# Loading the mixer's output weights ahead of a modulation group, and moving conv taps and weight splits from VectorE to GpSimd

## The chip, the cores and the metric

The kernel runs on one core of one Trainium2 chip. The metric is device time in microseconds, the median over runs.

## The reference

One call computes a first block (batch 1, 512 positions, model width 1024), then two further layers with attention (8 forgetting heads and 8 sparse heads), each with a gated feed-forward. The change touches the first block most:

```
cond = silu(c) @ ada_w + ada_b          # shift1, scale1, gate1, shift2, scale2, gate2
h = modulate(rmsnorm(x), shift1, scale1)
u, v, val, gate = split(h @ w_in + b_in)
y_a = gelu(u) * spatial(layernorm(gelu(v)))            # chunks of 128 positions
y_b = silu(channel_norm(conv31(val * sigmoid(gate))))  # causal depthwise conv, 512 channels
y = concat(rmsnorm(y_a), rmsnorm(y_b))
x = x + gate1 * (y @ w_out)
h2 = modulate(rmsnorm(x), shift2, scale2)
x = x + gate2 * ((silu(h2 @ w_gate) * (h2 @ w_up)) @ w_down)
```

All weights and activations are float32.

## The kernel before

**Activations** stand transposed: 1024 channels are eight tiles of 128 partitions, 512 positions are the free axis. `X0` to `X3` hold the residual (two channel tiles each), `H0` to `H7` the operand of the next matmul, each with a hi part (written by ACT) and a lo part (by DVE).

**Products.** Each float32 product is three matmuls: hi weight by hi and by lo activation, lo weight by hi activation. `Weights` (`W`) does the weights: `plan` queues a slab's spec, `load` (L299 to L318) issues one DMA of 512 KB into `raw`, and `split` lets ACT copy it to `wh` and DVE subtract to get `wl`; with the flag `pool` of the spec, GpSimd subtracts. `take` hands out a slab and then keeps `look` = 4 ready; `ahead(n)` loads and splits until n are ready. All slabs share a ring of 37 buffers with other tiles, so that a load can wait for a buffer to come free; SP's queue issues the DMAs in order.

**Modulation.** `ada_fetch` issues slabs of ada_w (`adaw`, 512 KB); `ada_group` uses eight of them, 32 small matmuls, ends with `adasb` and a transposing pair, and fetches ahead for the next group. Groups run once after `spatial`, then at m == 2 and m == 5 of the loop over w_out's first half (called second and third group).

**The conv** runs two channel tiles at a time over 31 lags. In `conv`, lags below `nd` are DVE operations into PSUM (`ax`), the others an ACT scale into `tap` (two buffers) and a GpSimd addition into `cv`. `center` then adds `ax` to `cv` on DVE, and statistics, `z`, silu and H4 to H7 follow.

**The output projection.** The loop over m takes slabs 0 to 3 of w_out (rows of H0 to H3); the second half takes slabs 4 to 7 (H4 to H7) by halves of 256 positions, adds into X, sums squares (`sq`, `st`), and `normed` makes H0 to H7 of the next norm from X and the reciprocal `rsw`. Then the first feed-forward begins with the tiles of gate and up, of 24 matmuls each.

**Order.** Parts outside `Ordered` are placed by a scheduler; a wrapper at L113 records every instruction, so that the rows of the profile all read L113 and are told apart by tile names. `uT` is the gated spatial part, from which H0 to H3 come; `sp` its PSUM-side operand.

Of the kernel before, what the change touches and what calls it, by code (L numbers as in the profile page):

```python
# [48 lines left out]
BK = 0  # L49
HP = 300  # L50
ND0 = 23
ND1 = 17
ND = (ND0, ND1)
PP0 = 1
PP1 = 6
# [3 lines left out]
PP5 = 2  # L59
PP = (PP0, PP1, PP2, PP3, PP4, PP5)  # L60
WP = 0
UP = 0
PY = 4
PZ = 4
GNV = False
# [55 lines left out]
def body(ctx: ExitStack, tc: tile.TileContext, I: dict, out, dbg=None):  # L121
# [28 lines left out]
    def MM():  # L150
        return ps.tile([P, S], F32, tag="mm", name="mm", bufs=4)
# [186 lines left out]
    W = Weights(4)  # L338
    W.pool = True

    def rows_of(w, k0, kt, c0, n):
        return w[k0 * P:(k0 + kt) * P, c0:c0 + n].rearrange("(k p) m -> p k m", p=P)

    def plan_cols(w, k0, kt, c0, n):
        W.plan([(0, P, 0, n, rows_of(w, k0, kt, c0, n))], kt, n)
# [9 lines left out]
    for c in range(4):  # L355
        plan_cols(w_in, 0, 8, c * P, P)
    for k0 in (0, 4):
        for g in range(4):
            plan_cols(I["w_out"][0], k0, 4, g * HS, HS)

# [15 lines left out]
    def plan_ffn(gate, up, down, pool=False):  # L376
        def gu(m):
            plan_cols(gate, 0, 8, m * P, P)
            plan_cols(up, 0, 8, m * P, P)

        def dn(m, k0, kts):
            for kt in kts:
                plan_cols(down, k0, kt, m * P, P)
                k0 += kt
        for m in range(KF0 + 1):
            W.pool = pool and m < 4
            gu(m)
        for m in range(KD - 1):
            dn(m, 0, (7, 7))
        for m in range(KF0 + 1, KF):  # L390
            gu(m)
        dn(KD - 1, 0, (7, 7))
        for m in range(KD):
            dn(m, KF0, (8,))

    plan_ffn(I["w_ffn_in"][0][:, :FF], I["w_ffn_in"][0][:, FF:], I["w_ffn_out"][0], UP)

    awi = I["attn_w_in_2"][0]
    FQ, FK, FV, FFG, NQ, KC, VC, KS, VS, KW, VW, NG = 0, 512, 1024, 1536, 1544, 2056, 2184, 2312, 2440, 2568, 2696, 2824
    plan_cols(awi, 0, 8, KC, P)  # L400
    plan_cols(awi, 0, 8, VC, P)
    plan_cols(awi, 0, 8, KS, P)
    plan_cols(awi, 0, 8, KW, P)
    for k0, kt in ((0, 3), (3, 3), (6, 2)):
        W.plan([(0, P, 0, 128, rows_of(awi, k0, kt, VS, 128)), (0, P, 128, 256, rows_of(awi, k0, kt, VW, 128)),
                (0, P, 256, 264, rows_of(awi, k0, kt, FFG, 8)), (0, P, 264, 288, rows_of(awi, k0, kt, NG, 24))], kt, 288)
# [206 lines left out]
    def pump(n, m=0):  # L613
        owed[0] += n
        owed[1] += m
        n, m = int(owed[0]), int(owed[1])
        owed[0] -= n
        owed[1] -= m
        for j in range(max(n, m)):
            if j < m and bp:  # L620
                bp.popleft()()
            if j < n and bg:
                bg.popleft()()
# [25 lines left out]
    def ada_group(ahead):  # L649

        pq = MM()
        for k in range(KD):
            ada_fetch(1)
            a, col, bias, _ = adal.popleft()
            for j in range(4):
                TE.matmul(pq[32 * j:32 * j + 32, :HS], lhsT=c32[:, k, :], rhs=a[:, j // 2, (j % 2) * HS:(j % 2 + 1) * HS],
                          start=(k == 0), stop=(k == KD - 1))
        ada_columns(pq, col, bias)
        ada_fetch(ahead)
# [265 lines left out]
    def factor(acc_, bank=ST):  # L925

        rsb = ACC()
        act(rsb, stats(acc_, 0, S, 512, bank=bank), AF.Copy)
        return rsb
# [243 lines left out]
    def out_mm(o, k0, slab, e, c0, c1):  # L1173
        wh, wl, _ = slab
        cs = slice(e * P, (e + 1) * P)
        for k in range(4):
            HO.mm3(o, k0 + k, wh[:, k, cs], wl[:, k, cs], c0, c1, k == 0, k == 3)

    def gated(m, o, c0, c1, rsb, eng):
        t = T()[:, :c1 - c0]  # L1180
        stt(t, o, mod[:, 16 + m:17 + m], rsb[:, c0:c1], OP.mult, OP.mult)
        eng.tensor_tensor(x_(m, c0, c1), x_(m, c0, c1), t, op=OP.add)
# [10 lines left out]
    for m in range(KD):  # L1193
        oa.append(MM())
        out_mm(oa[m], 0, gets(m // 2)[0], m % 2, 0, S)
        if m == LA:
            fa = factor(accA)
        if m >= LA:
            for x in range(0 if m == LA else m, m + 1):
                gated(x, oa[x], 0, S, fa, G if GA else V)  # L1200
        pump(PY, PP[5])
        if m in (2, 5):
            ada_group(ADN if m == 2 else 2)
    pump(len(bg))
# [575 lines left out]
```

## Time and profile before

| | before |
|---|---|
| median of 3 runs | 1676.74 us (1675.54 to 1678.24) |
| profiled execution | 1677.02 us |
| its span | 1675.3 us |
| PE, DVE, ACT, POOL busy | 1635.3, 882.7, 680.8, 129.3 us |
| granted TensorE clock, mean | 0.993 of full speed |

PE is TensorE's matmuls, DVE VectorE, ACT ScalarE, POOL GpSimd, SP the engine that issues most DMAs. Times in the rows are counted from the span's start. The profiled execution is 1.72 us longer than its span.

### The profile page before, as it was taken

The numbers are of one execution on the slowest core, as the hardware profiler recorded it, in microseconds if no ns is written. First come the engines' busy times: TensorE is split into PE (matmuls) and PEld (weight loads), VectorE is DVE, ScalarE is ACT, GpSimd is POOL, SyncE is SP. The second block draws the span as 40 slices with busy tenths as digits, with TensorE's granted clock in tenths as the row PEclk, the third lists the DMA queues.
The fourth block names the chain that finished last, engine by engine and source line by source line (L and its number), as shares of the span: only waits on it lengthen the run. The fifth ranks groups of instructions, "written<-read, shape, count | busy, mean of one in ns | idle before, by whom it ended". The sixth has DMA issues, their size and how long they took to land.

```text
span 1675.3 us, 22098 instructions
## 1 busy us (share of the span) xinstructions
PE 1635.3 (98%) x8797; PEld 1361.0 (81%) x8797; DVE 882.7 (53%) x1645; ACT 680.8 (41%) x1232; POOL 129.3 (8%) x144
## 2 busy tenths in 40 slices
PE   7999999999999999999999999999998999999998
PEld 4885798887888998777778988888887998888886
DVE  5798584444333584778766444323258734441244
ACT  4685352222222364455557323213236822322232
POOL 0452000000000011100101000000012100000002
PEclk9999999999999999999999999999999999999999
DMA  9634445544532433311134232234221532232511
GB/s 304 178 129 174 151 113 176 158 145 126 157 96 63 111 67 79 89 39 39 38 101 126 68 97 76 88 113 139 88 76 51 139 89 76 76 125 90 150 39 51
DMA packets 245168, 179.55 MB, mean 107 GB/s; under 512 B 20688, under 2 KB 220224, under 8 KB 245064
## 3 DMA queue, kind: packets, MB, share of 16 engines
q1 hardware_dynamic: 240520, 176.99, 36.0%
q10 hardware_dynamic: 4544, 1.14, 0.4%
q8 instruction: 69, 1.13, 0.3%
q14 instruction: 35, 0.29, 0.1%
HBM read 175.99 MB, written 2.11 MB: 106 GB/s over the span
## 4 chain that ended last, share of the span: by engine, by line
PE 86%; DVE 3%; ACT 2%; DMA 1%; issue 1%; SPq 0%; DVEq 0%; ACTq 0%
PE mm L113 79%; PE st L113 3%; PE ax L113 3%; DVE wl L113 0%; DVE pw L113 0%; DMA raw<-in_w_out_dram 0%; ACT pw L113 0%; ACT sq L113 0%; DVE H L113 0%; DVE XT L113 0%; DMA raw<-in_ffn_w_up_dram 0%; ACT pt L113 0%; DVE mg L113 0%; DVE lg L113 0%; DVE fk L113 0%
## 5 line engine op out<-in xcount | busy, mean ns | idle before, releaser
L113 PE MATMUL mm<-H,wh 128*128 128x512 f32 (+1 forms) x3168 | 872.6, 362 | 8.2 <-ACT wh L113 2.9
L113 PEld LDWEIGHTS mm<-H,wh 128*128 128x128 f32 x3168 | 566.2, 190 | 105.6 <-issue 5.4
L113 PE MATMUL mm<-H,wl 128*128 128x512 f32 (+1 forms) x1584 | 569.5, 361 | 3.0 <-DVE wl L113 2.9
L113 DVE TENSOR_TENSOR wl<-raw,wh 128x1024 fp32r<-128x1024 f32 (+1 forms) x257 | 309.4, 1220 | 217.5 <-ACT wh L113 202.3
L113 PEld LDWEIGHTS mm<-H,wl 128*128 128x128 f32 x1584 | 300.5, 190 | 47.9 <-DVE wl L113 3.6
L113 ACT ACTIVATE wh<-raw 128x1024 fp32r<-128x1024 f32 (+1 forms) x257 | 262.1, 1041 | 121.1 <-PE mm L113 49.1
L113 PE MATMUL mm<-wh,hid 128*128 128x512 f32 x704 | 217.5, 389 | 0.0
L113 DVE TENSOR_TENSOR silu<-silu,mm 128x512 f32<-128x512 f32 (+1 forms) x77 | 47.0, 611 | 249.3 <-PE mm L113 245.3
L113 PEld LDWEIGHTS mm<-wh,hid 128*128 128x128 f32 x704 | 132.1, 188 | 27.4
L113 ACT ACTIVATE hid<-silu 128x512 fp32r<-128x512 f32 (+1 forms) x77 | 43.8, 569 | 242.2 <-DVE silu L113 234.5
L113 PE MATMUL mm<-wl,hid 128*128 128x512 f32 x352 | 137.3, 390 | 0.0
L113 PE MATMUL mm<-hid,wh 128*128 128x512 f32 (+1 forms) x464 | 116.3, 340 | 0.0
L113 PEld LDWEIGHTS mm<-hid,wh 128*128 128x128 f32 x464 | 80.3, 190 | 9.9 <-issue 0.4
L113 POOL TENSOR_TENSOR mg<-mg,gb 128x512 f32<-128x512 f32 x32 | 44.2, 1387 | 467.0 <-ACT sq L113 458.4
L113 ACT ACTIVATE silu<-silu 128x512 f32<-128x512 f32 (+1 forms) x52 | 29.3, 565 | 123.3 <-DVE silu L113 123.2
L113 PE MATMUL mm<-hid,wl 128*128 128x512 f32 (+1 forms) x232 | 79.1, 341 | 0.0
L113 PEld LDWEIGHTS mm<-wl,hid 128*128 128x128 f32 x352 | 66.1, 188 | 13.8 <-DVE wl L113 0.3
L113 DVE TENSOR_TENSOR silu<-mm,rsb 128x512 f32<-128x512 f32 (+1 forms) x52 | 31.6, 608 | 73.1 <-PE mm L113 72.6
L113 PE MATMUL mm<-wh,H 128*128 128x512 f32 (+2 forms) x256 | 66.0, 345 | 2.8 <-ACT wh L113 1.6
L113 DVE TENSOR_TENSOR hid<-silu,hid 128x512 fp32r<-128x512 f32 (+1 forms) x77 | 47.3, 614 | 37.4 <-ACT hid L113 37.3
L113 POOL TENSOR_TENSOR cv<-cv,tap 128x488 f32<-128x488 f32 (+12 forms) x40 | 52.5, 1347 | 87.3 <-ACT cv L113 70.3
L113 ACT ACTIVATE silu<-mm 128x512 f32<-128x512 f32 (+1 forms) x25 | 13.7, 546 | 110.4 <-PE mm L113 110.4
(271 smaller groups left out, 1634.9 us busy)
## 6 DMA issues: line engine op xcount, KB each, us to landing
adaw<-in_ada_w_dram SPq DMA_DIRECT2D x48, 512.0 KB
raw<-in_w_ffn_in_dram SPq DMA_DIRECT2D x44, 512.0 KB
raw<-in_ffn_w_gate_dram SPq DMA_DIRECT2D x44, 512.0 KB
raw<-in_ffn_w_up_dram SPq DMA_DIRECT2D x44, 512.0 KB
raw<-in_ffn_w_down_dram SPq DMA_DIRECT2D x44, 512.0 KB
raw<-in_w_in_dram SPq DMA_DIRECT2D x16, 512.0 KB
adaw<-in_ada_f_w_dram SPq DMA_DIRECT2D x16, 512.0 KB
raw<-in_attn_w_in_dram SPq DMA_DIRECT2D x16, 512.0 KB
```

Of the source, the lines that this page charges most:

```text
L113: ins = f(*a, **k)
```

## The change

`ND1` goes from 17 to 14: for the second pair of channel tiles, lags 14, 15 and 16 of each tile move from DVE to ACT and GpSimd. `W.ahead(6)` ahead of the second group puts slabs 4 to 7 of w_out ahead of the slabs which that group fetches for the third. The flag `pool` is set for w_out's slabs 4 to 7, for the gate and up slabs of m < 4 of the first feed-forward (`UP` = 1) and for four slabs of the attention's input projection.

```diff
-ND1 = 17
+ND1 = 14
...
-UP = 0
+UP = 1
...
     for k0 in (0, 4):
+        W.pool = k0 == 4
         for g in range(4):
             plan_cols(I["w_out"][0], k0, 4, g * HS, HS)
...
+    W.pool = True
     plan_cols(awi, 0, 8, KC, P)
     plan_cols(awi, 0, 8, VC, P)
     plan_cols(awi, 0, 8, KS, P)
     plan_cols(awi, 0, 8, KW, P)
+    W.pool = False
...
         pump(PY, PP[5])
+        if m == 2:
+            W.ahead(6)
         if m in (2, 5):
             ada_group(ADN if m == 2 else 2)
```

SP's queue from the first w_out slabs to the first feed-forward slabs, as the difference of the two orders (L309 is `load`, L636 or L639 `ada_fetch`):

```order
 L309 DMA raw<-in_w_out_dram 128x4x256 x4
-L636 DMA adaw<-in_ada_w_dram 128x1024 x8
-L309 DMA raw<-in_w_out_dram 128x4x256 x2
-L636 DMA adaw<-in_ada_w_dram 128x1024 x8
-L309 DMA raw<-in_w_out_dram 128x4x256 x2
+L639 DMA adaw<-in_ada_w_dram 128x1024 x8
+L309 DMA raw<-in_w_out_dram 128x4x256 x4
+L639 DMA adaw<-in_ada_w_dram 128x1024 x8
```

Slabs 6 and 7 have moved ahead of the third group's eight `adaw` slabs.

DVE where H3 of the mixer is made, as the difference (`ax_1175` and `ax_1213` are the two tiles of the pair, `wl_1222` is slab 3, `H3_93` the lo part):

```order
 L113 SCALAR_TENSOR_TENSOR ax_1175<-glu_291,fixed_69,ax_1175 128x499
+L113 SCALAR_TENSOR_TENSOR ax_1213<-glu_291,fixed_69,ax_1213 128x499
+L113 TENSOR_TENSOR cv_289<-cv_289,ax_1175 128x512
+L113 TENSOR_TENSOR wl_1222<-raw_1219,wh_1221 128x1024
 L113 SCALAR_TENSOR_TENSOR H3_93<-uT_1043,fixed_69,H3_93 128x512
-L113 SCALAR_TENSOR_TENSOR ax_1213<-glu_291,fixed_69,ax_1213 128x499
-L113 TENSOR_TENSOR wl_1222<-raw_1219,wh_1221 128x1024
 L113 TENSOR_TENSOR acc_1260<-acc_1260,sq_1324 128x512
```

The addition of the first tile's `ax` into `cv`, which waits for GpSimd's last tap of that tile, and slab 3's split now stand ahead of H3's lo part.

PE where the first feed-forward begins, first before (`mm_2148` and `mm_2149` are the first gate and up tile, `mm_2216` the next gate tile):

```order
L113 MATMUL mm_2148<-H5_95,wh_1743 128x256
L113 MATMUL mm_2148<-H5_95,wl_1744 128x256
L113 MATMUL mm_2149<-H4_94,wl_1750 128x256
L113 MATMUL mm_2149<-H5_95,wh_1749 128x256 x2
L113 MATMUL mm_2149<-H5_95,wl_1750 128x256
L113 MATMUL mm_2216<-H0_90,wh_1755 128x256 x2
L113 MATMUL st_1946<-sq_2120,fixed_69 128x256
L113 MATMUL mm_2148<-H6_96,wh_1743 128x256
L113 MATMUL mm_2149<-H6_96,wh_1749 128x256
L113 MATMUL mm_2216<-H0_90,wl_1756 128x256
```

and of the change (`mm_2160` is the first gate tile, `mm_2161` the first up tile):

```order
L113 MATMUL mm_2160<-H5_95,wh_1755 128x256 x2
L113 MATMUL mm_2160<-H5_95,wl_1756 128x256
L113 MATMUL mm_2160<-H6_96,wh_1755 128x256 x2
L113 MATMUL mm_2160<-H6_96,wl_1756 128x256
L113 MATMUL mm_2160<-H7_97,wh_1755 128x256
L113 MATMUL mm_2161<-H0_90,wh_1761 128x256
L113 MATMUL mm_2160<-H7_97,wh_1755 128x256
L113 MATMUL mm_2160<-H7_97,wl_1756 128x256
```

The first gate tile is no longer interleaved with the next two; one matmul of another tile is left among its last ones.

## Rows read from the trace of the kernel before

**Rows 1.** The page's first line and its busy time by engine (share of the span, instructions).

```profile
span 1675.3 us, 22098 instructions
PE 1635.3 (98%) x8797; PEld 1361.0 (81%) x8797; DVE 882.7 (53%) x1645; ACT 680.8 (41%) x1232; POOL 129.3 (8%) x144
```

**Rows 2.** The timeline of PE: start, us, engine, operation, and in brackets the idle time before with what released it. The last row is from 383 to 389 us, the others from 189.9 to 204.

```profile
194.53 0.70 PE L113 MATMUL st<-sq,fixed 128*128 128x256 f32 x2 [0.50 <-ACT sq L113]
198.10 1.01 PE L113 MATMUL mm<-H,wh 128*128 128x256 f32 x3 [2.87 <-ACT wh L113]
...
201.04 0.63 PE L113 MATMUL mm<-H,wh 128*128 128x256 f32 x2
...
201.68 0.63 PE L113 MATMUL mm<-H,wh 128*128 128x256 f32 x2
...
385.19 0.79 PE L113 MATMUL mm<-H,wl 128*128 128x512 f32 x1 [2.86 <-DVE wl L113]
```

**Rows 3.** The chain of waits that ended last, between 176 and 206 us: start, us, what.

```profile
188.79 1.43 SPq L636
...
190.27 6.70 DMA raw<-in_w_out_dram
...
196.99 1.06 ACT wh L113
```

**Rows 4.** Windows: from and to, length, busy time (instructions) of PE, PEld, DVE, ACT and POOL, granted PE clock, DMA share, GB/s.

```profile
190.90:204.00 13.10, 9.73 (x49) 8.59 (x49) 6.24 (x14) 3.45 (x6) 0.00 (x0) 0.75 0.71 208
204.00:230.00 26.00, 25.88 (x194) 24.84 (x193) 23.01 (x45) 13.34 (x26) 0.00 (x0) 1.00 0.36 101
230.00:240.00 10.00, 10.00 (x85) 10.00 (x84) 8.17 (x16) 6.18 (x11) 0.00 (x0) 1.00 0.40 110
```

**Rows 5.** The timeline of SP's queue, which issues the slabs, 120 to 200 us.

```profile
137.80 2.21 SPq L309 DMA_DIRECT2D raw<-in_w_out_dram  x2
178.08 12.14 SPq L636 DMA_DIRECT2D adaw<-in_ada_w_dram  x8
190.27 0.98 SPq L309 DMA_DIRECT2D raw<-in_w_out_dram  x2
```

**Rows 6.** The timeline of PE, 137 to 191 us.

```profile
140.65 0.50 PE L113 MATMUL mm<-H,wh 128*128 128x512 f32 x1 [1.29 <-DVE H L113]
...
142.67 0.58 PE L113 MATMUL mm<-H,wh 128*128 128x512 f32 x1
...
150.67 1.66 PE L113 MATMUL mm<-H,wh 128*128 128x512 f32 x6
...
185.78 0.95 PE L113 MATMUL ax<-fixed,acc 128*128 128x1 f32 x8
...
187.29 0.49 PE L113 MATMUL ax<-fixed,rs 128*128 128x128 f32 x2
```

**Rows 7.** The timeline of ACT, 128 to 164 us.

```profile
139.32 1.27 ACT L113 ACTIVATE tap<-glu,fixed 128x482 f32<-128x482 f32 x2
...
145.62 0.36 ACT L113 ACTIVATE adasb<-mm 128x256 f32<-128x256 f32 x1
```

**Rows 8.** The timeline of DVE, 128 to 192 us.

```profile
134.76 3.38 DVE L113 TENSOR_TENSOR uT<-uT,sp 128x512 f32<-128x512 f32 x2
138.07 0.74 DVE L113 SCALAR_TENSOR_TENSOR sp<-mm,fixed,bvs 128x512 f32<-128x512 f32 x1
...
143.41 0.68 DVE L113 TENSOR_TENSOR uT<-uT,sp 128x512 f32<-128x512 f32 x1
...
149.19 0.75 DVE L113 SCALAR_TENSOR_TENSOR H<-uT,fixed,H 128x512 fp32r<-128x512 f32 x1
...
150.50 1.22 DVE L113 TENSOR_TENSOR wl<-raw,wh 128x1024 fp32r<-128x1024 f32 x1
...
162.19 0.68 DVE L113 TENSOR_TENSOR cv<-cv,ax 128x512 f32<-128x512 f32 x1
```

**Rows 9.** The timeline of POOL, 118 to 164 and 609 to 617 us, and from the page the group of its `mg` operations (busy, mean ns of one).

```profile
129.56 1.04 POOL L113 TENSOR_TENSOR cv<-cv,tap 128x485 f32<-128x485 f32 x1 [5.95 <-ACT tap L113]
132.37 5.22 POOL L113 TENSOR_TENSOR cv<-cv,tap 128x484 f32<-128x484 f32 x4 [1.77 <-ACT tap L113]
140.15 2.79 POOL L113 TENSOR_TENSOR cv<-cv,tap 128x482 f32<-128x482 f32 x2 [2.55 <-ACT tap L113]
...
615.01 0.39 POOL L113 CAST ks<-ks 64x256 fp32r<-64x256 f32 x1 [472.07 <-ACT ks L113]
...
L113 POOL TENSOR_TENSOR mg<-mg,gb 128x512 f32<-128x512 f32 x32 | 44.2, 1387 | 467.0 <-ACT sq L113 458.4
```

**Rows 10.** The timeline of DVE, 194 to 238 us.

```profile
213.93 1.74 DVE L113 RECIPROCAL rsw<-sdw 128x256 f32<-128x256 f32 x1
215.59 1.16 DVE L113 TENSOR_TENSOR wl<-raw,wh 128x1024 fp32r<-128x1024 f32 x1
...
232.44 0.38 DVE L113 SCALAR_TENSOR_TENSOR H<-t,fixed,H 128x256 fp32r<-128x256 f32 x1
```

**Rows 11.** The timeline of PE, 203.5 to 238 us.

```profile
212.67 0.70 PE L113 MATMUL st<-sq,fixed 128*128 128x256 f32 x2
...
217.58 0.70 PE L113 MATMUL st<-sq,fixed 128*128 128x256 f32 x2
...
218.24 0.40 PE L113 MATMUL mm<-H,wh 128*128 128x256 f32 x2
```

## The prediction

> **What bounds the kernel now.** I read the share of each engine first [rows 1]: PE is busy for 1635.3 of 1675.3 us, so whatever is to be won lies in PE's idle time, its clock, or work taken from it, and this change takes no work from PE. I therefore listed PE's idle pieces in the stretch that the change rearranges, 120 to 240 us. The largest stands at 198.10, 2.87 us behind an ACT split [rows 2]; 0.50 us stands at 194.53. The chain around that stall [rows 3] names its origin: SP's queue is busy issuing the third modulation group's slabs until 190.22, the output slab of w_out is issued only at 190.27, takes 6.70 us to land, and its split by ACT ends at 198.05. Last the windows by stage [rows 4]: from 190.9 to 204 the granted clock averages 0.75, from 204 on it is 1.00. The PE rows after the stall show the lower of the two levels, 1.2 GHz: a matmul of 256 columns starts every 0.21 us at 201.04 to 201.68 where it starts every 0.12 us from 230 to 240.
>
> So the late slab costs 0.50 + 2.87 us idle, and the 5.8 us from 198.1 to 203.9 at half clock do the work of 2.9 us: **6.3 us in all**, out of 40 that PE is idle in the whole span.
>
> **W.ahead(6).** SP's queue is in order. Before, slabs 6 and 7 stand behind the third group's eight `adaw` slabs, and the first of those waited until 178.08 [rows 5]. In the changed order all of w_out precedes them. Slab 5 now waits for a buffer until the second add into X1 (before: issued at 137.80), which stands on DVE behind the normalised conv output, about 174; slabs 6 and 7 follow about 176 and 177, the group's slabs from 178, as before. At 12.14 us for eight [rows 5], 1.5 each, the six that this group's result needs have been issued by 187, and PE wants the last near 190. Slabs 5 to 7 are needed from 192 on and are then 14 us old. I count the whole 6.3 us: **-6.3**. If the slabs were again late by as much, it would be 0.
>
> One smaller loss comes with it. In the changed PE order the group's 24 matmuls no longer stand around the `ax` statistics, so that between the sums and the broadcast of their reciprocal nothing fills the way over ACT and DVE: the sums ended at 186.73, the broadcast began at 187.29 [rows 6]; with the hand-over back to PE **+0.7**.
>
> **Three more taps a tile on Pool.** This takes six operations from DVE and puts six ACT taps of 0.64 us and six Pool adds into 137 to 155 [rows 7, 9]. What matters is order. On ACT, four taps now stand between `adasb` (ends 145.98 [rows 7]) and the split of slab 3 and the hi part of H3. On DVE the addition `cv<-cv,ax`, which needs Pool's last tap of its tile, now stands ahead of slab 3's split and of the lo part of H3; before it came at 162.19, long after Pool had finished at 142.94 [rows 8, 9]. By hand: taps on ACT from 146.0 to 148.5; their Pool adds take 1.04 us alone to 1.31 (5.22 for four) beside DVE [rows 9], first one from 146.6, so the fourth ends at 150.8 to 151.9; then the addition 0.6, the split 1.15 (1.22 less what overlaps [rows 8]), at worst another Pool add of 1.0 in between, and H3's lo 0.75: 153.3 to 155.4, instead of 149.94. PE has 13 matmuls that don't need it, 0.23 us each from 150.67, hence until 153.7 [rows 6]. The stall is 0 to 1.7 us; I take **+1.1**, nearer to the end with Pool and DVE in each other's way, because that is how these rows look now (uT below). PE was sent to half clock here once already, at 142.67, after a wait of 1.29 us at 140.65 [rows 6]; if it happens again it costs another 1.5.
>
> Slab 3's load now waits for the third uT addition (about 144.1) and the second group's eight slabs stand behind it, the third of them behind the acc addition after H3 (155.4). PE uses that one about 161 and the others 2 us apart, against 1.5 us on the queue. I cost it at nothing; by a landing of 6.70 us [rows 3] it would be 1.
>
> **Splits on Pool.** The order shows 16: four of w_out, eight of the first feed-forward slabs, four in the attention input. Price of one: the trace has no 128x1024 operation on Pool. Two taps of 485 columns are 2.1 us; two `mg` of 128x512 at 1.387 are 2.8 [rows 9]. I take 2.4, against 1.21 on DVE [rows 8]. Pool is empty from 142.94 to 615.01 [rows 9], so its own time is free; what isn't is DVE's. `uT<-uT,sp`, two operands in SBUF, takes 1.69 us each while Pool adds taps and 0.68 after; `sp<-mm`, with one operand in PSUM, keeps 0.74 at 138.07 beside it [rows 8]. So a DVE operation with two SBUF operands loses about 1.0 us to a Pool add of 1.31: three quarters of it, 1.85 us of a split of 2.4.
>
> The Trainium skill, "SBUF — State Buffer", section "SBUF: two separate sides", is stricter: the port pair is an exclusive lock, and the one that starts second waits for the other's whole instruction. By that, each split costs the full 2.4.
>
> Where this counts is the way to the first feed-forward matmul. Before, DVE is busy without a gap from the reciprocal at 213.93 to H7's lo part at 232.82 [rows 10], 18.9 us, of which four splits like that at 215.59 take 1.1 each and a second reciprocal 1.7 like the first; the changed order has neither ahead of H7, which leaves 12.8. PE before had 24 matmuls of the next tile `mm_2149` and some of `mm_2216` to fill the waits for H4 to H7; in the changed order `mm_2160` stands alone, with one matmul of fill. From the last statistics matmul to H7's use PE has 104 matmuls at 0.118 and 7 `st` at about 0.54 (0.66 from 217.58 to 218.24 with one matmul [rows 11]), 16.1 us; the reciprocal started 1.3 after that point (212.67 [rows 11] to 213.93), so DVE has 14.8 us for 12.8: slack 2.0. Three Pool splits fall into it: the first beside the reciprocal, 0.7 of it left over, two others 1.85 each, 4.4; less 2.0 is **+2.4**. By the quoted rule it is 0.7 + 4.8 - 2.0 = 3.5, and the sum would be 1.1 higher. If Pool blocks nothing it is 0; if all three block 2.8 in full, 6.4.
>
> The w_out and later feed-forward splits are loaded four slabs ahead and I cost them at nothing; PE takes 2.9 us for a 24-matmul slab, longer than Pool needs. Nor the attention's four: PE shows no idle there that a split ends; without that cover 4 x 1.2 = 4.8. The second large stall, 385.19 [rows 2], stays: the order there is the same.
>
> **Sum.** -6.3 + 0.7 + 1.1 + 2.4 = -2.1. On the profiled execution (1677.02, of which 1675.3 is the span [rows 1]) that is 1674.9; the median shown is 0.28 lower, so **1674.6**.
>
> **Rivals.**
> - *The slab gain arrives whole*: Pool blocks DVE for less than the 2.0 us of slack, H3 is in time. -6.3 + 0.7 to 1.1: 1671 to 1672, at most 1673.3. For it: ten splits at 1.22, 12 us, leave DVE where it is full. Chance 0.36.
> - *Slower, by the port*: the three splits around H3 to H7 block in full, 8.4 - 2.0 = 6.4, and the waiting sends PE to half clock as at 198.10, 2.9 more. -6.3 + 0.7 + 1.1 + 9.3 = +4.8: 1681.5. It decides once those splits hold DVE for over 7 us with the clock down. For it: the lone `mm_2160`; against: three in a row must each hit a two-operand instruction. Chance 0.16, with what the same mechanism does in the second half's H chain.
> - *The change doesn't do what it says*: slabs 6 and 7 wait for X buffers until about 185 and the group is later too; 0 + 0.7 + 1.1 + 2.4 = +4.2: 1680.9. Against: the queue orders them by adds that run at 174 to 177. Chance 0.06.
> - *My case*, given back in part, 1673.4 to 1678: chance 0.42.
>
> **Numbers.** A measurement of this kernel tells about 0.2% (3.35 us) from nothing: below 1673.4 is faster, above 1680.1 slower. Faster 0.36, same 0.43, slower 0.21. The range takes in the whole gain (-5.6 with one loss, 1671) and stops at 1681, short of the port's worst.
>
> **What would show it.** Right: no wait for `wh` near 198 and granted clock 1.00 from 190 to 205; `raw<-in_w_out_dram` issued x4 ahead of the third group; a PE wait for DVE H near 154; `wl` on Pool at 2.1 to 2.8 us and X, t or H on DVE at up to 2 us beside it; PE waits for DVE H of some 2 us in sum ahead of the first 24 matmuls of the feed-forward. Wrong: a PE wait for `adaw` near 160 or 190, a half-clock stretch behind H3 or H7, or DVE at its own pace beside Pool's splits.

## The result and the profile after

| | before | after |
|---|---|---|
| median | 1676.14 us (6 runs) | 1691.29 us (1687.55 to 1696.53, 6 runs) |
| profiled execution, its span | 1677.02, 1675.3 us | 1691.96, 1690.2 us |

The ratio is 1.0093 with a 95% interval of 1.0076 to 1.0110: the change makes the kernel slower by 13 to 18 us. I had forecast 1674.6 with a range that ended at 1681.

The page of the changed kernel, its first line, the busy time by engine, and the group of GpSimd's splits (busy, mean ns of one, idle before):

```profile
span 1690.2 us, 22130 instructions
...
PE 1640.7 (97%) x8797; PEld 1363.7 (81%) x8797; DVE 887.1 (52%) x1623; ACT 685.4 (41%) x1238; POOL 178.3 (11%) x166
...
L113 POOL TENSOR_TENSOR wl<-raw,wh 128x1024 fp32r<-128x1024 f32 x16 | 40.0, 2501 | 409.0 <-ACT wh L113 409.0
```

Sixteen splits left DVE, and DVE is busy for 4.4 us **longer** than in [rows 1], although sixteen splits of 1.22 and six taps are gone from it. That is the first sign: other DVE operations became longer by more than what was taken away. PE is idle for 49.5 us in place of 40.

The windows of the changed kernel, in the columns of [rows 4]:

```profile
160.00:181.40 21.40, 21.40 (x154) 13.55 (x147) 10.97 (x17) 7.52 (x12) 1.90 (x1) 0.88 0.47 164
...
190.90:204.00 13.10, 9.81 (x87) 6.40 (x86) 2.36 (x7) 2.19 (x4) 2.36 (x1) 0.81 0.96 335
204.00:230.00 26.00, 22.50 (x157) 21.11 (x157) 19.22 (x34) 11.18 (x21) 9.56 (x4) 0.96 0.34 87
```

From 160 to 181.4 the granted clock is 0.88; before, the same window reads:

```profile
160.00:181.40 21.40, 21.40 (x142) 14.10 (x142) 16.73 (x26) 8.89 (x14) 0.00 (x0) 1.00 0.11 33
```

From 204 to 230 PE lacks 3.5 us of work where it lacked 0.12 in [rows 4]. The timeline of PE names what it waits for:

```profile
151.65 0.73 PE L113 MATMUL mm<-H,wh 128*128 128x512 f32 x2 [1.11 <-DVE fixed L113]
...
156.17 0.50 PE L113 MATMUL mm<-H,wh 128*128 128x512 f32 x1 [1.27 <-DVE H L113]
...
190.33 0.39 PE L113 MATMUL mm<-H,wh 128*128 128x256 f32 x1 [2.71 <-DVE H L113]
...
197.55 0.64 PE L113 MATMUL mm<-adaw,fixed 128*32 128x256 f32 x8 [1.13 <-DMA adaw<-in_ada_w_dram]
...
201.72 0.69 PE L113 MATMUL st<-fixed,adasb 128*128 128x128 f32 x2 [0.51 <-ACT adasb L113]
...
215.00 0.70 PE L113 MATMUL st<-sq,fixed 128*128 128x256 f32 x2 [1.08 <-ACT sq L113]
...
226.64 0.70 PE L113 MATMUL st<-sq,fixed 128*128 128x256 f32 x2 [1.68 <-ACT sq L113]
...
399.59 0.50 PE L113 MATMUL mm<-H,wl 128*128 128x512 f32 x1 [2.86 <-DVE wl L113]
```

Three marks of PE's timeline make a ledger. The first two rows are of the kernel before, the next two of the change: the start of w_out's second half, and the first matmul with slab 5.

```profile
181.40 0.40 PE L113 MATMUL mm<-H,wh 128*128 128x256 f32 x2
190.91 0.49 PE L113 MATMUL mm<-H,wh 128*128 128x256 f32 x2
```

```profile
186.27 0.40 PE L113 MATMUL mm<-H,wh 128*128 128x256 f32 x2
202.06 0.78 PE L113 MATMUL mm<-H,wh 128*128 128x256 f32 x2
```

The second half of w_out began at 181.40 before and begins at 186.27: 4.9 late. The first matmul with slab 5 began at 190.91 before and begins at 202.06: 11.2 late. The stall behind DVE's split stood at 385.19 [rows 2] and stands at 399.59: 14.4 late, of the 14.9 by which the spans differ. So nearly all of the loss arises between 137 us and the first tiles of the feed-forward, in three stretches: the conv's end (+4.9), the third group (+6.3), and the H chain (from X to the H of the next norm), where the 6.3 us of slab 6's stall went away and 9.5 came in their place.

DVE beside GpSimd, first GpSimd's splits, then DVE's operations of the same times:

```profile
179.50 2.76 POOL L113 TENSOR_TENSOR wl<-raw,wh 128x1024 fp32r<-128x1024 f32 x1 [23.93 <-ACT wh L113]
183.42 2.95 POOL L113 TENSOR_TENSOR wl<-raw,wh 128x1024 fp32r<-128x1024 f32 x1 [1.17 <-ACT wh L113]
187.34 2.39 POOL L113 TENSOR_TENSOR wl<-raw,wh 128x1024 fp32r<-128x1024 f32 x1 [0.96 <-ACT wh L113]
...
223.08 2.38 POOL L113 TENSOR_TENSOR wl<-raw,wh 128x1024 fp32r<-128x1024 f32 x1 [3.85 <-ACT wh L113]
```

```profile
179.97 2.83 DVE L113 TENSOR_TENSOR acc<-acc,sq 128x512 f32<-128x512 f32 x1
182.73 0.74 DVE L113 SCALAR_TENSOR_TENSOR t<-mm,fixed,acc 128x512 f32<-128x512 f32 x1
...
184.05 2.87 DVE L113 TENSOR_TENSOR acc<-acc,sq 128x512 f32<-128x512 f32 x1
...
187.45 2.83 DVE L113 SCALAR_TENSOR_TENSOR H<-cv,fixed,H 128x512 fp32r<-128x512 f32 x1
...
212.40 0.48 DVE L113 SCALAR_TENSOR_TENSOR t<-mm,fixed,acc 128x256 f32<-128x256 f32 x1 [2.06 <-PE mm L113]
...
223.23 2.51 DVE L113 SCALAR_TENSOR_TENSOR t<-X,fixed,rsw 128x256 f32<-128x256 f32 x1
```

Four of these rows (179.97, 184.05, 187.45, 223.23) are DVE operations with two operands in SBUF that start during a split of GpSimd. Each ends 0.3 to 0.55 us after the split: H of 0.75 us takes 2.83, `t` of 0.47 takes 2.51. The `t` at 212.40, with one operand in PSUM (`mm`), keeps its 0.48 during a split that runs from 211.82 to 214.22. PE's wait of 2.71 us at 190.33 is that H. The waits for `st<-sq` are the same thing one step on: an add into X that waited for GpSimd, or stood on DVE behind an operation that did, its square on ACT, and PE behind the square. There are six of them from 210 to 239 us, 6.4 us in sum.

### The profile page after: what moved, and what is told of

Read it like the earlier page. It is cut to its first block, busy times and chain, and to the rows that moved or that the text cites. A ratio compares the mean times of both kernels' runs of the same rounds, so it can differ in the third digit from the quotient of the medians.

```text
span 1690.2 us, 22130 instructions
## 1 busy us (share of the span) xinstructions
PE 1640.7 (97%) x8797; PEld 1363.7 (81%) x8797; DVE 887.1 (52%) x1623; ACT 685.4 (41%) x1238; POOL 178.3 (11%) x166
## 4 chain that ended last, share of the span: by engine, by line
PE 81%; DVE 6%; ACT 2%; issue 1%; DMA 1%; SPq 0%; DVEq 0%; ACTq 0%
PE mm L113 75%; PE st L113 3%; PE ax L113 3%; DVE H L113 1%; DVE t L113 1%; DVE X L113 1%; ACT sq L113 1%; DMA adaw<-in_ada_w_dram 1%; DVE acc L113 0%; DVE wl L113 0%; DVE pw L113 0%; ACT H L113 0%; ACT pw L113 0%; DVE lg L113 0%; DVE XT L113 0%
## 5 line engine op out<-in xcount | busy, mean ns | idle before, releaser
L113 DVE TENSOR_TENSOR wl<-raw,wh 128x1024 fp32r<-128x1024 f32 (+2 forms) x241 | 291.5, 1226 | 207.8 <-ACT wh L113 182.9
L113 POOL TENSOR_TENSOR wl<-raw,wh 128x1024 fp32r<-128x1024 f32 x16 | 40.0, 2501 | 409.0 <-ACT wh L113 409.0
L113 POOL TENSOR_TENSOR cv<-cv,tap 128x488 f32<-128x488 f32 (+15 forms) x46 | 61.9, 1377 | 90.6 <-ACT cv L113 70.3
```

What stands on the lines that cost most here:

```text
L113: ins = f(*a, **k)
```

## The experiments

All times below are medians beside the medians of before on the same chip, with the interval of the ratio.

| kernel | median | before | ratio (95%) |
|---|---|---|---|
| no_pool | 1680.12 | 1675.80 | 1.0023 (1.0011 to 1.0035) |
| no_taps | 1689.67 | 1675.80 | 1.0092 (1.0072 to 1.0111) |
| no_ahead | 1690.10 | 1675.80 | 1.0088 (1.0070 to 1.0106) |
| ahead_only | 1679.78 | 1675.80 | 1.0025 (1.0015 to 1.0035) |
| no_ffn_pool | 1684.98 | 1675.72 | 1.0048 (1.0034 to 1.0062) |
| no_wout_pool | 1685.61 | 1676.31 | 1.0054 (1.0042 to 1.0066) |
| attn_pool_only | 1676.70 | 1676.31 | 1.0008 (0.9997 to 1.0018) |
| taps_only | 1679.47 | 1676.31 | 1.0019 (1.0009 to 1.0029) |
| dummy_sub | 1694.30 | 1675.72 | 1.0106 (1.0091 to 1.0122) |
| dummy_after | 1675.30 | 1676.31 | 0.9991 (0.9979 to 1.0002) |
| dummy_set | 1684.09 | 1675.72 | 1.0046 (1.0033 to 1.0059) |
| fetch_split | 1672.94 | 1675.72 | 0.9974 (0.9963 to 0.9984) |

**Undoing one part.** `no_pool` is the change without every `W.pool` line and with `UP = 0`; `no_taps` has ND1 = 17; `no_ahead` lacks the two lines of `W.ahead(6)`; `ahead_only` is before with those two lines alone.

```diff
+        if m == 2:
+            W.ahead(6)
         if m in (2, 5):
```

> The change without its 16 splits on GpSimd: three more taps a tile and the early load of slabs 4 to 7 stay. Theory P (GpSimd's splits hold DVE's operations with two SBUF operands): the wait of 2.71 us for H at 190.33 and the waits for st<-sq and H from 207 to 242 go, some 11 us: 1680. Theory T (the taps make everything late): only 3 us come back, 1688. Theory A (the early load makes the third group late): 1686 to 1688.

> The change with ND1 = 17 again: GpSimd's splits and the early load stay. Theory P: only the lateness that stands before the first split goes, 4.9 us by the start of the second half of w_out (186.27 against 181.40): 1686.5. Theory T: 1675 to 1678, as nothing is late any more. Theory A: 1686.

> The change without W.ahead(6): slabs 6 and 7 stand behind the third group again. Theory A: the waits for adaw at 197.55 to 200.14 and what follows go, and the time falls to 1680 or below. Theories P and T: the stall for slab 6 comes back, but is partly hidden behind the other waits: 1690 to 1695.

> Before, with W.ahead(6) alone. Theories P and T, and the sum of the prediction: -6.3 for slab 6's stall and its half clock, +0.7 for the statistics without fill: 1670.5. Theory A: the slabs put ahead of the third group make PE wait for adaw instead: 1676 to 1682.

Without the splits on GpSimd 4.3 us are left of some 15: these splits cost 11 in the medians, as theory P has it (in the two profiled executions the stall near 385 stands 15.5 us apart, 384.11 and 399.59). Neither undoing the taps nor undoing the early load brings back more than 2 us of the median. For `no_taps` all three forecasts missed (1675 to 1686.5, measured 1689.67); its profiled execution, the fastest of five, stands at 393.02 at the stall, 6.6 us ahead of the change, so what the taps cost inside the change stays open. And `ahead_only` contradicts P and me: it is 4.0 us slower than before, not 5.6 faster. Its SP queue; slab 6's issue in a narrower window; two pieces of its chain of waits; and PE:

```profile
137.49 43.94 SPq L309 DMA_DIRECT2D raw<-in_w_out_dram  x4
181.48 4.88 SPq L636 DMA_DIRECT2D adaw<-in_ada_w_dram  x8
```

```profile
177.59 0.37 SPq L309 DMA_DIRECT2D raw<-in_w_out_dram  x1
```

```profile
180.34 0.70 DVE acc L113
...
181.06 0.37 SPq L309
```

```profile
188.24 0.64 PE L113 MATMUL mm<-adaw,fixed 128*32 128x256 f32 x8 [1.22 <-DMA adaw<-in_ada_w_dram]
...
194.95 0.69 PE L113 MATMUL st<-fixed,adasb 128*128 128x128 f32 x2 [0.50 <-ACT adasb L113]
...
383.99 0.79 PE L113 MATMUL mm<-H,wl 128*128 128x512 f32 x1 [2.86 <-DVE wl L113]
```

The queue stands ahead of slab 6 until an add into X on DVE is done (issue at 177.59), then ahead of slab 7 until DVE's addition `acc` ends at 181.04 (issue at 181.06), and reaches the third group at 181.48 in place of 178.08 [rows 5]. PE waits for one `adaw` after the other, 3.3 us in sum, and comes to slab 5 at 195.29, 4.4 later than before. From there to the stall at 383.99 it needs 188.7 us in place of 194.3: **the 6.3 us that I read off were there, all but 0.7, and 4.4 of them were paid ahead.** In `no_pool` it is 188.0, the whole 6.3, after an arrival 5.2 late.

At that mark `ahead_only` is 1.2 us ahead of before; its span is 1.7 us longer. Matched row by row with before, its lag goes from -1.2 to +0.1 between 385.19 and 390.0, and from +0.8 to +2.1 between 692 and 702.5: both times around a wait of PE, with the lower clock behind it. What sets the length of these stretches stays open, and so does how much of the 4.0 us of the medians they explain.

**Which splits.** `no_ffn_pool` is the change with `UP = 0`, `no_wout_pool` the change without `W.pool = k0 == 4`, `attn_pool_only` before with the attention's flag alone.

> The change with UP = 0: the first feed-forward's eight splits go back to DVE; w_out's four and the attention's four stay on GpSimd. If GpSimd's splits cost where they stand, the waits for st<-sq from 207 to 242 go and the wait of some 2.7 us for H before the ax sums stays: 1682 to 1685, between the change (1691) and the change without any split on GpSimd (1680). If w_out's splits are the whole cost: 1690. If the feed-forward's are: 1680.

> The change with w_out's slabs 4 to 7 split on DVE again; the feed-forward's eight and the attention's four stay on GpSimd. Without the feed-forward's eight it was 1685.0, without any 1680.1. If the parts add up, w_out's four cost some 5 us beside the attention's share and this gives 1686; if the feed-forward's eight alone are enough for the whole loss, since the same PE waits follow: 1690.

> Before with the four attention slabs on GpSimd alone. The prediction costs them at nothing: 1676. If they hold DVE as the others do: 4 x 1.9 us of waiting DVE, of which PE shows at most a part: 1677 to 1680.

Beside the 4.3 us of `no_pool`, w_out's four (with the attention's) make 9.3, the feed-forward's eight (with the attention's) make 9.3 too: 5.0 each, and the two make 10 of the 11, each uncertain by some 3 us by the intervals. The attention's four are 0.4 us, not to be told from nothing. So the splits cost where DVE's adds and H operations are on PE's way, on average about 1.2 us for each of w_out's and 0.6 for each of the feed-forward's, and nothing that shows for the attention's.

**The taps alone.**

```diff
-ND1 = 17
+ND1 = 14
```

> Before with ND1 = 14 alone. The prediction's term was +1.1: 1677. By the rows of the change, PE stands 4.9 us later at the start of w_out's second half (186.27 against 181.40), and nothing after it gives this back: 1680 to 1681. If PE then waits for the third group or slab 6 in any case and the lateness is absorbed: 1676 to 1677.

Slower by 3.2 us (1.5 to 4.9), more than the prediction's term or its absorption, less than the reading from the rows of the change. The timeline of PE in `taps_only`:

```profile
149.15 0.50 PE L113 MATMUL mm<-H,wh 128*128 128x512 f32 x1 [1.09 <-DVE H L113]
...
152.48 0.73 PE L113 MATMUL mm<-H,wh 128*128 128x512 f32 x2 [1.11 <-DVE fixed L113]
...
156.99 0.50 PE L113 MATMUL mm<-H,wh 128*128 128x512 f32 x1 [1.25 <-DVE H L113]
...
200.93 0.62 PE L113 MATMUL mm<-H,wh 128*128 128x256 f32 x3 [1.48 <-ACT wh L113]
...
385.52 0.50 PE L113 MATMUL mm<-H,wl 128*128 128x512 f32 x1 [2.86 <-DVE wl L113]
```

Three waits in place of the one that I had priced, and DVE's rows at the first two say why:

```profile
147.40 1.69 DVE L113 SCALAR_TENSOR_TENSOR H<-uT,fixed,H 128x512 fp32r<-128x512 f32 x1
149.02 1.71 DVE L113 TENSOR_TENSOR acc<-acc,sq 128x512 f32<-128x512 f32 x1
150.65 1.70 DVE L113 TENSOR_TENSOR uT<-uT,sp 128x512 f32<-128x512 f32 x1
```

GpSimd's later taps hold three more operations, of H2, acc and uT, for a microsecond each. They make the second half of w_out 4.2 us late (185.61 against 181.40). But in this execution the lateness is gone again by the stall near 385 (385.52, before 385.19): the wait for slab 6 shrank from 2.87 to 1.48 us, without the stretch at the lower clock. So the absorbed reading is right up to there, and where the median's 3.2 us arise stays open. Taps (+3.2) and early load (+4.0) together make +4.3, not 7.2, in the medians. The traces fit that, since both make PE late at the same place: the first matmul with slab 5 comes 4.2 us late with the taps, 4.4 with the early load, and 5.2 with both.

**Is it the port, or the late `wl`?** In `dummy_sub` DVE makes every split as before, and GpSimd computes the same subtraction into a tile that nobody reads. `dummy_after` has GpSimd busy in the same places, reading only eight columns of SBUF each time. In both, PE, DVE and ACT have the order of before, instruction by instruction.

```diff
+                    V.tensor_tensor(fl(wl), fl(raw), fl(wh).bitcast(F32), op=OP.subtract)
+                    if pool:
+                        G.tensor_tensor(dummy[:, :n], fl(raw), fl(wh).bitcast(F32), op=OP.subtract)
```

In `dummy_after` the last line is instead:

```diff
+                        G.tensor_copy(dummy[:, :8], fl(wh)[:, :8].bitcast(F32))
+                        for _ in range(2):
+                            G.memset(dummy[:, :n], 0.0)
```

> Before, with DVE making every split as before, and GpSimd computing the same subtraction a second time into a tile that nobody reads, for w_out's slabs 4 to 7 and the feed-forward's first eight. Nobody waits for GpSimd's result. Theory P, the port: DVE's operations with two SBUF operands still wait for whole GpSimd operations, and DVE has its splits besides: 1686 or more. Theory L (what costs is that wl comes 2.4 us after wh and not 1.2, and later): 1676 to 1677, as before.

> As dummy_sub, in the same places, but GpSimd copies eight columns of wh (which makes it wait for ACT's split) and then sets the unread tile to zero twice: busy at the same time, hardly reading SBUF. PE, DVE and ACT have the order of before. If DVE is held by GpSimd's operands: 1676 to 1679, as before. If any GpSimd operation that writes SBUF holds DVE: towards dummy_sub's 1694.

> As dummy_sub, but GpSimd sets the tile to zero twice in place of the subtraction, so that it is busy and reads no SBUF. Theory P with a port that is held by reads of two operands: 1676 to 1678. If any activity of GpSimd holds DVE: as dummy_sub, less as far as its operations are shorter. Theory L: 1676 to 1677.

Nobody needs GpSimd's result in `dummy_sub` (one buffer that it held delayed ACT by 0.6 us), and it loses 18 us, more than the change; DVE has its splits besides. GpSimd and DVE in `dummy_sub`:

```profile
222.35 4.02 POOL L113 TENSOR_TENSOR dummy<-raw,wh 128x1024 f32<-128x1024 f32 x1 [4.23 <-ACT wh L113]
```

```profile
222.56 1.22 DVE L113 TENSOR_TENSOR wl<-raw,wh 128x1024 fp32r<-128x1024 f32 x1
...
224.03 2.62 DVE L113 SCALAR_TENSOR_TENSOR H<-t,fixed,H 128x256 fp32r<-128x256 f32 x1
```

It goes both ways: GpSimd's 2.4 us became 4.02 beside DVE's split at 222.56, and DVE's H became 2.62 behind GpSimd. In `dummy_after`:

```profile
215.29 1.81 POOL L113 COPY dummy<-wh 128x8 f32<-128x8 f32 x1 [2.70 <-ACT wh L113]
...
221.71 1.97 POOL L113 MEMSET dummy<- 128x1024 f32 x2
```

```profile
222.70 0.42 DVE L113 TENSOR_TENSOR X<-X,t 128x256 f32<-128x256 f32 x1
```

Setting a tile to zero twice, 1.97 us in all, GpSimd lets the X add and its neighbours through at 0.42 to 0.48 us, and the time is that of before. One thing besides GpSimd differs from before in both dummies: SP's queue comes to slabs 6 and 7 sooner than at 190.27. First `dummy_sub`, then `dummy_after`, each with its stall near 385:

```profile
185.34 1.15 SPq L311 DMA_DIRECT2D raw<-in_w_out_dram  x2
...
400.83 0.61 PE L113 MATMUL mm<-H,wl 128*128 128x512 f32 x1 [2.86 <-DVE wl L113]
```

```profile
183.83 1.02 SPq L311 DMA_DIRECT2D raw<-in_w_out_dram  x2
...
380.83 0.61 PE L113 MATMUL mm<-H,wl 128*128 128x512 f32 x1 [2.86 <-DVE wl L113]
```

So the two are better compared with each other than with before: they issue these slabs within 1.5 us of each other, and 20 us lie between their stalls, 19 between their medians. That `dummy_after` ends with the time of before, though it stood 4.4 us ahead at the stall, doesn't show that zeroing is free in all; DVE's rows show that it doesn't hold them. So theory L falls (in the change itself, too, no wait of PE ends with a `wl` of GpSimd; in `no_ahead` one does, 1.19 us), and what costs is GpSimd reading its operands while DVE reads two. `dummy_set` failed as a control: its zeroing waited for nothing and ran in the first 26 us, where PE then waited 7.29 us at 30.69; it says nothing on the question.

**The early load at the right place.** Of the eight `adaw` slabs that are fetched at m == 2, the third group needs six. `fetch_split` puts slabs 6 and 7 of w_out behind the sixth.

```diff
-            ada_group(ADN if m == 2 else 2)
+            ada_group(ADN - 2 if m == 2 else 2)
+            if m == 2:
+                W.ahead(6)
+                ada_fetch(ADN)
```

> Before, with slabs 6 and 7 put behind the sixth adaw slab of the eight, the last that the third group needs, in place of ahead of all or behind all. The group is not delayed, and slab 6 is issued two slabs sooner, 3 us at 1.5 each: the stall of 2.87 us and part of the 2.9 us at half clock go, 1671 to 1674. If what ahead_only lost came from elsewhere than the group's delay: 1676 to 1680.

```profile
178.00 3.07 SPq L636 DMA_DIRECT2D adaw<-in_ada_w_dram  x6
181.16 0.96 SPq L309 DMA_DIRECT2D raw<-in_w_out_dram  x2
```

```profile
190.64 0.44 PE L113 MATMUL st<-fixed,adasb 128*128 128x128 f32 x2 [0.51 <-ACT adasb L113]
...
378.08 0.50 PE L113 MATMUL mm<-H,wl 128*128 128x512 f32 x1 [2.86 <-DVE wl L113]
```

```profile
190.90:204.00 13.10, 13.10 (x99) 12.62 (x98) 10.62 (x23) 5.26 (x11) 0.00 (x0) 1.00 0.49 148
```

The group's end is where it was (190.64, before 190.72), and from 190.9 to 204 PE is never idle and never at the lower clock, where [rows 4] had 9.73 busy and 0.75. The profiled execution, at 1668.31 us one of the three fastest of eleven, reaches the stall 7.1 us sooner; the medians differ by 2.8 us, the ratio is 0.9974 (0.9963 to 0.9984): **faster than before by 2.7 to 6.2 us, and than the change by about 18.** That the whole time gains less than the stall's 7.1 us stays unexplained.

## Why the prediction was wrong, step by step

- **Slab 6's stall, -6.3: right in size, wrong in what it costs to remove.** `fetch_split` shows the gain by itself. The step that failed is "slabs 6 and 7 follow about 176 and 177, the group's slabs from 178, as before": they were issued at 177.6 and 181.1 in `ahead_only`, at 182.8 and 187.6 in the change, and the whole group stood behind. The buffer of slab 7 came free in `ahead_only` with DVE's addition `acc` at 181.04, not with an add into X at 177, though nothing delayed DVE there: I had read the queue's order and took the wrong addition for its last buffer. In the change, GpSimd's split held `acc` until 186.92, and the add into X behind it released slab 7. I also gave the two slabs ahead of the group no time: the group began 3.4 us later in `ahead_only` and ended 4.2 later (194.95 against 190.72).
- **No fill around the statistics, +0.7: right** (a wait of 0.57 us in the change and in `ahead_only`).
- **Taps, +1.1: mis-sized.** They made the second half of w_out 4.2 us late by themselves and cost 3.2 in the median. I priced the one instruction that the order put behind GpSimd's last tap (its wait was 1.27), and not the three operations ahead of it that later taps slow down as well, nor the lower clock that followed (0.88 from 160 to 181 in the change). Nor did I see that part of it is absorbed by the wait for slab 6 where that wait is left in.
- **Second group behind slab 3, nothing: right**; PE shows no wait for `adaw` near 160.
- **Price of a split on GpSimd, 2.4: right**, 2.50 measured.
- **Three quarters of it is lost by DVE: somewhat low.** The four operations above that met a split lost 2.0 to 2.2 us each where I took 1.85, so 0.6 to 1.0 us more for three splits. The trace agrees with the Trainium skill here: the rule of "SBUF — State Buffer", section "SBUF: two separate sides", is that the second waits for the first's whole instruction, and H at 187.45 ends 0.55 us after the split that ends at 189.73. One row I misread on the way: `sp<-mm` at 138.07 doesn't run beside a tap, since GpSimd is idle there from 137.59 to 140.15 [rows 9]; that an operand in PSUM spares an operation is shown by the `t` at 212.40 instead.
- **"Three Pool splits fall into it": this is the step that broke the forecast.** I asked where PE waits for `wl`, found four slabs of look-ahead, and cost the other splits at nothing. But a split on GpSimd costs by the DVE operation that it hits, not by its own result. Of w_out's four, three hit two additions into acc and H7 (2.83 to 2.87 each), and the fourth found DVE idle; the first six of the feed-forward hit adds into X, a `t` and an H, and PE waited for squares six times. With all of them the splits cost 11 us where I had 2.4; the rival "slower, by the port" had the mechanism and 9.3 us of price, but for three splits around H3 to H7 only.
- **The attention's four, nothing: right** (0.4 us, not measurable).

By rows of the change the sum is 4.9 (conv) + 6.3 (third group, of which 2.7 is H7 behind GpSimd) - 6.3 (slab 6) + 9.5 (X, H and the clock behind GpSimd: six waits of 6.4 in sum; the rest isn't taken apart, and the granted clock was 0.96 from 204 to 230) = 14.4, as measured at 399.59. The 9.5 is what is left when the other terms are taken from 14.4; `no_pool` checks it, with 188.0 us from slab 5 to the stall against 197.5 in the change.

## What to carry to other kernels

An idle engine is not free when reading its operands holds up a busy one: price a move to it by the operations of the other engine that it will hit and by who waits for those, not by the idle share nor by who waits for the moved result. A load is put ahead of others in an in-order queue only as far as its own buffer is free by then; behind the last transfer that is needed sooner it cost that group nothing here. When a stall is removed, look at which transfers were waiting behind it: here the fix was a matter of two slabs in the order.

## What the runs showed of the hardware that I had not expected

- GpSimd is held by DVE too: a copy of eight columns took 0.19 us alone and 1.81 beside DVE's split and the X add behind it, and a subtraction of 2.4 us took up to 4.02.
- Zeroing a tile on GpSimd, 1.97 us for two in a row, left DVE's two-operand operations at their own 0.42 to 0.48 us.
- The lower clock after the same wait of 2.86 us near 385 cost 1.3 us more in `ahead_only` than before, and the wait near 700 another 1.3: a gain can be given back at places that the edit does not touch.
